# Weight-stationary projections for x, B and C in a hybrid SSD / attention trunk, with edits to the score order and the last product

## The chip, the cores and the metric

One core of one Trainium2 chip runs the whole kernel. The metric is the device time of one execution in microseconds. Three runs of the kernel before gave 2508.55 to 2509.58 us, with a median of 2509.29 us.

## The reference

Two layers over 256 tokens of width 2048, each followed by a SwiGLU feed-forward block; RMSNorm before and after every block, everything in float32.

```python
for i in range(DEPTH):                                   # DEPTH = 2
    h = rmsnorm(x, norm_mix_pre[i])
    if i % 2 == 0:
        m = ssd_mixer(h, ssd_w_in, conv_w, conv_b, dt_bias, a_log, d, norm, w_out)
    else:
        m = diff_attention(h, w_qkv, lq1, lk1, lq2, lk2, subln, w_out, lambda_init)
    x = x + rmsnorm(m, norm_mix_post[i])
    h = rmsnorm(x, norm_ffn_pre[i])
    x = x + rmsnorm((silu(h @ w_gate) * (h @ w_up)) @ w_down, norm_ffn_post[i])
```

`ssd_mixer` multiplies h by `w_in` and cuts the product into a gate z (4096 channels), x (4096), B and C (1024 each) and dt (64). x, B and C go through a causal depthwise convolution of width 4 over the tokens, then SiLU; then a chunked state-space scan, a gated group norm and an output product. `diff_attention` has 16 heads with two score maps each; the second map is subtracted with a weight lambda that comes from four vectors of 64.

## The kernel before, in words

Each matrix product in float32 is made of three float32r products: every operand is split into a high part (`hi`, rounded) and a low part (`lo`, the rest), and hi*hi, hi*lo and lo*hi are added up. Weights stream from memory in blocks of 512 input rows by 512 columns (1 MB); `prep` makes `hi` on ScalarE (a cast, L137) and `lo` on VectorE (a subtraction, L138). In the SSD layer a block is prepared in two halves, with four `hi` and four `lo` buffers in turn; from the attention on, four rows of 512 columns are prepared at once.

Two forms of product matter here.

- `mv` (matmul at L191): the activations are stationary (128 tokens at a time, t = 0 and 1) and the weights stream past, 512 columns at once. A chunk of 512 output columns with 2048 input rows takes 16 x 2 x 3 = 96 matmuls of 512 columns. The result has the tokens on the partitions. The two products of a step run with a lag, so that a chunk's second half of tokens ends inside the next chunk. Two PSUM banks (`acc`, four in all) are used.
- `ws` (matmuls at L239 and L241): the weights are stationary, 128 output channels at a time (`ct` = 0 to 3), and the activations stream: a matmul of 512 columns does hi weights against hi and lo of x for all 256 tokens, a second one of 256 columns does lo weights against hi of x. A chunk takes 16 x 4 = 64 pairs, and the result has the channels on the partitions. All four `acc` banks are used. Evacuation: ScalarE copies one half of the bank out (L1034), VectorE adds the other half (L1035) and, where wanted, multiplies by a row of token scales (L1038). Before the change only q and k of the attention use it.

In the SSD layer (0 to about 616 us) the chunks follow in this order: z0, B0, C0, x0, x1, z1, x2, x3, z2, z3, a first output product, then B1, C1, x4, x5, z4, z5, x6, x7, z6, z7. The twelve chunks of x, B and C go through `conv_chunk`: `mv`, evacuation with the token's scale (`tk`, ScalarE, L515), eight 128x128 transposes on TensorE to bring the channels to the partitions (`pc`, L509), then `conv_silu`, which reads the transposed data from PSUM: ScalarE makes `v` (L492), three scalar_tensor_tensor on VectorE add the shifted taps (L494), ScalarE takes a tanh (L497), VectorE makes the result (L498).

What is not a step of the main product is queued with `later(k, ...)`, which places it k steps further on (a step is half a block, 6 matmuls of each half of the tokens); `tick` runs what is due. The compiler's planner then sets the order on each engine; an engine works in that order. In an attention group, `later` places the scores, the softmax, the turning of the probabilities (transposes, L1091), the weighing of v (L1102) and the turning of the output (`piece`, L326).

At the end, the last product of the second feed-forward block runs as `mv` with the tokens t = 0 four steps ahead of t = 1. `norm_chain` then takes the row sums of squares (L337), a reciprocal root (L94, L97), and adds the scaled result to the residual stream in four pieces of 512 columns (L679, L680, L682), each written out by a DMA of the SP queue (L684).

Of the kernel before, what the change touches and what calls it, by code (L numbers as in the profile page):

```python
# [45 lines left out]
def trunk_kernel(ctx, tc, x_rows, x_cols, vec_cols, vec64, post_rows, lam_rows,  # L46
# [60 lines left out]
    def x_stat(kt, t):  # L107
        sl = slice(t * P, (t + 1) * P)
        return xT_hi[kt // 4][:, kt % 4, sl], xT_lo[kt // 4][:, kt % 4, sl]
# [68 lines left out]
            pending.popleft()()  # L178


    def mv(blocks, stat, evac, lag, scale=None, loaded=()):
        acc = {}
        last = 2 * len(blocks) - 1

        def run(i, t, hi, lo):
# [2 lines left out]
            for j in range(2):
                xh, xl = stat(i, j, t)
                for q, (a, b) in enumerate(((xh, hi), (xh, lo), (xl, hi))):  # L190
                    nc.tensor.matmul(acc[t], a, b[:, j], start=(i == 0 and j == 0 and q == 0),  # L191
                                     stop=(i == last and j == 1 and q == 2))
            if i == last:
# [306 lines left out]
    def conv_chunk(blocks, ch0, dst, then=None):  # L500

        tk = {}

        def conv():
            pcs = [aux("pc").rearrange("p (a s) -> p a s", a=2) for _ in range(2)]
            for t in (1, 0):
                for e, a in ((0, 0), (0, 1), (1, 0), (1, 1)):
# [1 line left out]
                    nc.tensor.transpose(pcs[e][:, a, t * P:(t + 1) * P], tk[t][:, cs], ident)  # L509
            for ct in range(4):  # L510
                conv_silu(pcs[ct // 2][:, ct % 2], ch0 + ct, dst(ct))

        def evac(t, ps):
# [1 line left out]
            nc.scalar.activation(tk[t], ps, AF.Copy, scale=rs0[t])  # L515
# [156 lines left out]
    def norm_chain(t, ss4, last_mw, step, final, t512):  # L672

        rn = rstd_of(ss4[:, 3:4], D, f"post{step}_{t}", ss4[:, 0:1])
        for n in range(4):
# [2 lines left out]
            if final and n == 0:
                nc.scalar.activation(mw, mw, AF.Copy, scale=rn)  # L679
                nc.gpsimd.tensor_tensor(xt, xt, mw, op=ALU.add)  # L680
            else:
                nc.vector.scalar_tensor_tensor(xt, mw, rn, xt, op0=ALU.mult, op1=ALU.add)  # L682
            if final:
                nc.sync.dma_start(out[t * P:(t + 1) * P, n * 512:(n + 1) * 512], xt)  # L684
# [314 lines left out]
    for e in range(2):
        nc.vector.tensor_tensor(lamv[:, 2 * e], lamv[:, 2 * e], lamv[:, 2 * e + 1], op=ALU.mult)  # L1000
        nc.vector.tensor_reduce(lsum[:, e:e + 1], lamv[:, 2 * e], axis=AX.X, op=ALU.add)
    nc.scalar.activation(lsum, lsum, AF.Exp)
# [194 lines left out]
```

## Time and profile before

| | |
|---|---|
| median of 3 runs | 2509.29 us (2508.55 to 2509.58) |
| the profiled execution's own time | 2509.47 us |
| its span | 2507.6 us |
| TensorE busy | 2489.6 us, 11818 matmuls |
| VectorE busy | 1936.8 us |
| ScalarE busy | 1403.2 us |
| GpSimd busy | 263.8 us |
| granted TensorE clock | 0.999 |

The 1.9 us between the span and the execution's own time lie around the program. A matmul's row shows its latency (389 ns for 512 columns), while successive matmuls start about 227 ns apart, so costs on TensorE are read from start to start, or from the chain of waits, which counts each piece once.

### The profile page before, as it was taken

The page shows a single profiled execution, that of the slowest core. Times are in us where ns is not written, and L with a number is a line of the kernel's source. Part 1 is how long each engine was busy: PE and PEld are TensorE (multiplying, and loading weights), DVE is VectorE, ACT ScalarE, POOL GpSimd, SP SyncE. Part 2 cuts the span into 40 slices and gives each one's busy share as a digit, 9 for nine tenths or more (in the row PEclk, how much of TensorE's full clock was granted, in tenths as well). Part 3 has the DMA queues.
Part 4 walks back from the last instruction along what each step waited for, and adds up shares of the span by engine and source line. Part 5 has one row for each costly group of instructions (what it writes and reads, how often), then busy time and mean ns, then how long its engine had stood idle before and what let it go on. Part 6 is the DMA issues. An engine that isn't in the chain of part 4 may idle for free.

```text
span 2507.6 us, 31493 instructions
## 1 busy us (share of the span) xinstructions
PE 2489.6 (99%) x11818; PEld 2062.5 (82%) x11818; DVE 1936.8 (77%) x2394; ACT 1403.2 (56%) x1895; POOL 263.8 (11%) x242
## 2 busy tenths in 40 slices
PE   9999999999999999999999999999999999999998
PEld 8888888888888888888888888888888888888886
DVE  6877547777688899978987766556688899879985
ACT  5767546665565455545554654455655465546553
POOL 0131000121110010001001100001100100020002
PEclk9999999999999999999999999999999999999999
DMA  7555555555786786868676544544776967686774
GB/s 287 195 171 199 185 191 195 175 179 192 255 275 202 253 256 215 256 209 265 217 247 237 185 171 144 199 167 143 255 234 207 289 223 232 217 265 225 224 247 151
DMA packets 143385, 541.43 MB, mean 216 GB/s; under 512 B 14400, under 2 KB 31104, under 8 KB 116224
## 3 DMA queue, kind: packets, MB, share of 16 engines
q1 hardware_dynamic: 125872, 503.96, 57.7%
q0 software_dynamic: 16992, 35.13, 7.1%
q8 instruction: 93, 1.52, 0.2%
q14 instruction: 60, 0.49, 0.1%
q10 hardware_dynamic: 368, 0.32, 0.1%
HBM read 520.41 MB, written 18.94 MB: 215 GB/s over the span
## 4 chain that ended last, share of the span: by engine, by line
PE 93%; DVE 2%; issue 1%; ACT 1%; DMA 1%; POOL 0%; SPq 0%; DVEq 0%; ACTq 0%; POOLq 0%
PE acc L265 38%; PE acc L191 33%; PE cp L265 9%; PE acc L239 5%; PE acc L241 2%; PE acc L216 2%; DVE lo L138 1%; PE pt_f L326 1%; ACT hi L137 1%; DMA raw<-in_w_g_dram 1%; PE py L607 1%; PE ptx L688 0%; PE po L1102 0%; PE pc L509 0%; PE px L594 0%
## 5 line engine op out<-in xcount | busy, mean ns | idle before, releaser
L138 DVE TENSOR_TENSOR lo<-raw,hi 128x2048 fp32r<-128x2048 f32 (+2 forms) x401 | 728.8, 1821 | 307.8 <-ACT hi L137 300.9
L137 ACT CAST hi<-raw 128x2048 fp32r<-128x2048 f32 (+2 forms) x401 | 604.6, 1511 | 432.9 <-PE acc L191 122.7
L191 PE MATMUL acc<-hi,xT 128*128 128x512 f32 x1792 | 570.3, 394 | 0.0
L265 PE MATMUL acc<-hi,xT 128*128 128x512 f32 x1608 | 518.7, 390 | 0.1
L191 PEld LDWEIGHTS acc<-hi,xT 128*128 128x128 f32 x1792 | 336.0, 188 | 71.4 <-issue 2.2
L265 PEld LDWEIGHTS acc<-hi,xT 128*128 128x128 f32 x1608 | 301.8, 188 | 63.0 <-DVE sx L748 0.5
L191 PE MATMUL acc<-lo,xT 128*128 128x512 f32 x896 | 351.9, 393 | 1.4 <-DVE lo L138 1.4
L265 PE MATMUL acc<-lo,xT 128*128 128x512 f32 x804 | 313.0, 389 | 0.0
L138 DVE TENSOR_TENSOR lo<-rawm,hi 128x2048 fp32r<-128x2048 f32 (+1 forms) x87 | 181.8, 2089 | 35.0 <-ACT hi L137 33.7
L137 ACT CAST hi<-rawm 128x2048 fp32r<-128x2048 f32 (+1 forms) x87 | 152.7, 1755 | 95.6 <-PE acc L265 54.6
L191 PEld LDWEIGHTS acc<-lo,xT 128*128 128x128 f32 x896 | 168.4, 188 | 37.3 <-DVE lo L138 4.9
L239 PE MATMUL acc<-xT,hi 128*128 128x512 f32 x512 | 181.2, 399 | 0.0
L265 PEld LDWEIGHTS acc<-lo,xT 128*128 128x128 f32 x804 | 150.9, 188 | 31.2
L265 PE MATMUL acc<-hi,ah_f 128*128 128x512 f32 x450 | 176.1, 391 | 0.0
L265 PE MATMUL acc<-hi,al_f 128*128 128x512 f32 x450 | 175.2, 389 | 0.0
L265 PE MATMUL acc<-lo,ah_f 128*128 128x512 f32 x450 | 175.1, 389 | 0.0
L265 PE MATMUL cp<-sh,ff 128*128 128x512 f32 x516 | 172.8, 389 | 0.0
L241 PE MATMUL acc<-xT,lo 128*128 128x256 f32 x512 | 142.9, 280 | 0.0
L142 DVE SCALAR_TENSOR_TENSOR lo<-raw,cols,hi 128x512 fp32r<-128x512 f32 x128 | 93.5, 774 | 56.9 <-ACT hi L141 56.5
L141 ACT ACTIVATE hi<-raw,cols 128x512 fp32r<-128x512 f32 x128 | 84.7, 716 | 64.1 <-PE acc L191 42.2
L239 PEld LDWEIGHTS acc<-xT,hi 128*128 128x128 f32 x512 | 96.1, 188 | 22.7
L265 PEld LDWEIGHTS cp<-sh,ff 128*128 128x128 f32 x516 | 96.9, 188 | 20.1
(305 smaller groups left out, 4081.5 us busy)
## 6 DMA issues: line engine op xcount, KB each, us to landing
raw<-in_w_zxbc_dram SPq DMA_DIRECT2D x77, 1024.0 KB, 4.8
raw<-in_w_d_dram SPq DMA_DIRECT2D x98, 512.0 KB, 5.8
raw<-in_w_g_dram SPq DMA_DIRECT2D x96, 512.0 KB, 6.5
raw<-in_w_u_dram SPq DMA_DIRECT2D x96, 512.0 KB, 5.9
raw<-in_w_qkv_dram SPq DMA_DIRECT2D x48, 1024.0 KB, 4.8
raw<-in_w_so_dram SPq DMA_DIRECT2D x32, 1024.0 KB, 4.8
rawm<-in_w_g_dram SPq DMA_DIRECT2D x64, 512.0 KB, 5.9
rawm<-in_w_u_dram SPq DMA_DIRECT2D x64, 512.0 KB, 6.1
```

The costliest lines, as they stand in the source:

```text
L137: nc.scalar.copy(hi, raw)
L138: nc.vector.tensor_tensor(lo, raw, hi.bitcast(F32), op=ALU.subtract)
L141: nc.scalar.activation(hi[:, j], raw[:, j], AF.Copy, scale=scale[j])
L142: nc.vector.scalar_tensor_tensor(lo[:, j], raw[:, j], scale[j], hi[:, j].bitcast(F32), op0=ALU.mult, op1=ALU.subtract)
L191: nc.tensor.matmul(acc[t], a, b[:, j], start=(i == 0 and j == 0 and q == 0), stop=(i == last and j == 1 and q == 2))
L216: nc.tensor.matmul(acc[job, t], a, b[:, j], start=(i == 0 and j == 0 and q == 0), stop=(i == last and j == 1 and q == 2))
L239: nc.tensor.matmul(acc[ct], hi[:, j, cs], x.rearrange("p a s -> p (a s)"), start=(i == 0 and j == 0), stop=False)
L241: nc.tensor.matmul(acc[ct][:, :S], lo[:, j, cs], x[:, 0], start=False, stop=(i == last and j == 1))
L265: nc.tensor.matmul(acc[k], a, b, start=first and q == 0, stop=last and q == 2)
L326: nc.tensor.transpose(pt[:, j], src[:, j * P:(j + 1) * P], ident)
L607: nc.tensor.matmul(py[e * 64:(e + 1) * 64, a], xd[c][:, 2 * a + e], mts[c][:, 2 * a + e], start=True, stop=True)
```

## The change

- `conv_chunk` calls `ws` in place of `mv`. Per block of 128 channels, ScalarE copies (`nc.scalar.copy`), VectorE adds and VectorE multiplies by `rstd_bc`, a row of token scales; the eight transposes and the `tk` evacuation go. `conv_silu` reads SBUF, not PSUM, and is queued one step earlier.
- The last product's last pair of K blocks, for t = 1, is split into two halves of 256 columns. What was summed before it is added to `m` first; each half is then evacuated, squared and multiplied on its own.
- At the very end all four pieces of the residual add are made on VectorE (before, the first was made by ScalarE and GpSimd), the last one in two halves, and two of the five DMAs are issued from ScalarE's queue.
- The preparation of lambda is queued 14 steps into the attention.
- In an attention group, the scores are placed one step later in three of the four groups (`k = hg < 3`), the three turnings of the probabilities are placed together, and so are the two weighings.

```diff
+    def mv(blocks, stat, evac, lag, scale=None, loaded=(), cut=False):
...
+            end = cut and i == last and t == 1
+            if end:
+                evac(t, acc[t])
+            for cs in (slice(0, 256), slice(256, 512)) if end else (slice(0, 512),):
+                if end:
+                    acc[t] = accp.tile([P, 512], F32, tag="acc", name="acc")
...
+                if end:
+                    evac(t, acc[t], cs)
...
         def conv():
-            pcs = [aux("pc").rearrange("p (a s) -> p a s", a=2) for _ in range(2)]
-            for t in (1, 0):
-                for e, a in ((0, 0), (0, 1), (1, 0), (1, 1)):
-                    cs = slice((2 * e + a) * P, (2 * e + a + 1) * P)
-                    nc.tensor.transpose(pcs[e][:, a, t * P:(t + 1) * P], tk[t][:, cs], ident)
             for ct in range(4):
-                conv_silu(pcs[ct // 2][:, ct % 2], ch0 + ct, dst(ct))
+                conv_silu(tk[ct], ch0 + ct, dst(ct))
-        def evac(t, ps):
-            tk[t] = s1.tile([P, 512], F32, tag="tk", name="tk")
-            nc.scalar.activation(tk[t], ps, AF.Copy, scale=rs0[t])
-            if t == NT - 1:
+        def evac(ct, ps, pl):
+            if ct % 2 == 0:
+                x = s1.tile([P, 2, S], F32, tag="tk", name="tk")
+                tk.update({ct + e: x[:, e] for e in range(2)})
+            x = tk[ct]
+            nc.scalar.copy(x, pl)
+            nc.vector.tensor_tensor(x, x, ps, op=ALU.add)
+            nc.vector.tensor_tensor(x, x, rstd_bc, op=ALU.mult)
+            if ct == 3:
                 later(1, conv)
...
-        mv(blocks, lambda i, j, t: x_stat(2 * i + j, t), evac, 1)
+        ws(blocks, evac)
...
-            if final and n == 0:
-                nc.scalar.activation(mw, mw, AF.Copy, scale=rn)
-                nc.gpsimd.tensor_tensor(xt, xt, mw, op=ALU.add)
-            else:
-                nc.vector.scalar_tensor_tensor(xt, mw, rn, xt, op0=ALU.mult, op1=ALU.add)
+            for cs in (slice(0, 256), slice(256, 512)) if final and n == 3 else (slice(0, 512),):
+                nc.vector.scalar_tensor_tensor(xt[:, cs], mw[:, cs], rn, xt[:, cs], op0=ALU.mult, op1=ALU.add)
+                if final:
+                    (nc.scalar if n % 2 and not cs.start else nc.sync).dma_start(
...
+            def halfway(t, ps, cs):
+                mt = m[(t, 3)]
+                nc.vector.tensor_tensor(mt[:, cs], mt[:, cs], ps[:, cs], op=ALU.add)
...
+                row_sumsq(sa, mt[:, cs], t512("junk")[:, cs])
...
+                nc.vector.tensor_tensor(last_mw[0][:, cs], mt[:, cs], pw(3)[:, cs], op=ALU.mult)
+                if cs.start:
+                    norm_chain(t, ss4[t], last_mw[0], step, final, t512)
...
+    later(14, lam)
...
-        later(2, all_scores)
-        later(6, lambda: turn(0, (0, 1)))
-        later(8, lambda: (turn(1, (0,)), weigh(0)))
-        later(10, lambda: turn(1, (1,)))
-        later(11, lambda: weigh(1))
-        later(13, lambda: (piece(0), piece(1)))
+        k = hg < 3
+        later(2 + k, all_scores)
+        later(9 + k, lambda: (turn(0, (0, 1)), turn(1, (0,)), turn(1, (1,))))
+        later(10 + k, lambda: (weigh(0), weigh(1)))
+        later(12 + k, lambda: (piece(0), piece(1)))
```

More of the change, by code (lines that the diff above doesn't have):

```diff
@@ L187, in run @@
                 acc[t] = accp.tile([P, 512], F32, tag="acc", name="acc")
[L188 to L193, printed above, removed]
+            end = cut and i == last and t == 1
[4 more added lines that the diff above has]
+                    acc[t] = accp.tile([P, 512], F32, tag="acc", name="acc")
+                for j in range(2):
+                    xh, xl = stat(i, j, t)
+                    for q, (a, b) in enumerate(((xh, hi), (xh, lo), (xl, hi))):
+                        nc.tensor.matmul(acc[t][:, cs], a, b[:, j, cs],
+                                         start=((i == 0 or end) and j == 0 and q == 0),
+                                         stop=(i == last - (cut and t == 1 and not end) and j == 1 and q == 2))
+                if end:
+                    evac(t, acc[t], cs)
+            if i == last and not end:
                 evac(t, acc[t])
@@ L677, in norm_chain @@
             xt = xres[(t, n)]
[L678 to L682 removed]
+            for cs in (slice(0, 256), slice(256, 512)) if final and n == 3 else (slice(0, 512),):
+                nc.vector.scalar_tensor_tensor(xt[:, cs], mw[:, cs], rn, xt[:, cs], op0=ALU.mult, op1=ALU.add)
+                if final:
+                    (nc.scalar if n % 2 and not cs.start else nc.sync).dma_start(
+                        out[t * P:(t + 1) * P, n * 512 + cs.start:n * 512 + cs.stop], xt[:, cs])
             if final:
[L684 removed]
                 continue
@@ L772, in out_proj, with evac @@
                     pw(n)
-            def evac(t, ps, n=n):
+            def halfway(t, ps, cs):
+                mt = m[(t, 3)]
+                nc.vector.tensor_tensor(mt[:, cs], mt[:, cs], ps[:, cs], op=ALU.add)
+                if cs.start == 0:
+                    last_mw.append(t512("mw"))
+                    sa = small.tile([P, 1], F32, tag="ss1", name="ssh", bufs=3)
+                else:
+                    sa = ss4[t][:, 3:4]
+                row_sumsq(sa, mt[:, cs], t512("junk")[:, cs])
+                if cs.start == 0:
+                    nc.vector.scalar_tensor_tensor(ss4[t][:, 0:1], sa, 1.0 / D, ss4[t][:, 0:1], op0=ALU.mult, op1=ALU.add)
+                nc.vector.tensor_tensor(last_mw[0][:, cs], mt[:, cs], pw(3)[:, cs], op=ALU.mult)
+                if cs.start:
+                    norm_chain(t, ss4[t], last_mw[0], step, final, t512)
+            last_mw = []
+            def evac(t, ps, cs=None, n=n):
+                if cs is not None:
+                    return halfway(t, ps, cs)
+                if final and n == 3 and t == 1:
+                    nc.vector.tensor_tensor(m[(t, n)], m[(t, n)], ps, op=ALU.add)
+                    return
                 if first:
@@ L799, in out_proj @@
             mv([w[n, kg // 2] for kg in up[::2]], up_stat, evac, LAG if last and n == 3 else lag,
-               (lambda i: [scale[:, 2 * up[i] + j:2 * up[i] + j + 1] for j in range(2)]) if scale is not None else None)
+               (lambda i: [scale[:, 2 * up[i] + j:2 * up[i] + j + 1] for j in range(2)]) if scale is not None else None,
+               cut=final and n == 3)
     for half in range(2):
@@ L995, in trunk_kernel, with lam @@
     make_causal_mask(nc, causal, NEG)
-    lamv = t512("lamv", (P, 4, 64))
-    nc.scalar.dma_start(lamv, lam_rows.partition_broadcast(P))
     lsum = const.tile([P, 2], F32, name="lsum")
[L999 to L1002, printed above, removed]
     neglam = const.tile([P, 1], F32, name="neglam")
-    nc.vector.tensor_tensor(neglam, lsum[:, 1:2], lsum[:, 0:1], op=ALU.subtract)
-    nc.vector.tensor_scalar(neglam, neglam, -LAMBDA_INIT, None, op0=ALU.add)
+    def lam():
+        lamv = t512("lamv", (P, 4, 64))
+        nc.scalar.dma_start(lamv, lam_rows.partition_broadcast(P))
+        for e in range(2):
+            nc.vector.tensor_tensor(lamv[:, 2 * e], lamv[:, 2 * e], lamv[:, 2 * e + 1], op=ALU.mult)
+            nc.vector.tensor_reduce(lsum[:, e:e + 1], lamv[:, 2 * e], axis=AX.X, op=ALU.add)
+        nc.scalar.activation(lsum, lsum, AF.Exp)
+        nc.vector.tensor_tensor(neglam, lsum[:, 1:2], lsum[:, 0:1], op=ALU.subtract)
+        nc.vector.tensor_scalar(neglam, neglam, -LAMBDA_INIT, None, op0=ALU.add)
+    later(14, lam)
     subc = const.tile([P, 1], F32, name="subc")
```

1 line of the change is left out of this document (removed).

## The prediction

> **What bounds the kernel now.** I read the page first (busy shares, slices, chain), then the chain of waits in one stretch at a time, then the groups by line and shape.
>
> ```profile
> span 2507.6 us, 31493 instructions
> PE 2489.6 (99%) x11818; PEld 2062.5 (82%) x11818; DVE 1936.8 (77%) x2394; ACT 1403.2 (56%) x1895; POOL 263.8 (11%) x242
> ...
> PE 93%; DVE 2%; issue 1%; ACT 1%; DMA 1%; POOL 0%; SPq 0%; DVEq 0%; ACTq 0%; POOLq 0%
> ```
>
> TensorE is the bound from end to end: 93% of the chain, and busy in 2489.6 of 2507.6 us. So a change pays by what it takes off TensorE's own sequence, by a wait on that sequence that it removes, or after the last matmul. All else is hidden as long as VectorE, the next busiest, keeps up. The profiled execution took 2509.47 us (its span and 1.9 us around it), 0.2 above the median of the runs, 2509.29; I make the sum against 2509.47 and take the 0.2 off at the end.
>
> A chunk of the old form and what follows it, in the chain of waits:
>
> ```profile
> 62.06 1.02 PE pc L509 x8
> 63.08 21.82 PE acc L191 x96
> 84.90 0.97 PE pc L509 x8
> ```
>
> The middle row is one whole chunk: 96 matmuls in 21.82 us, 227.3 ns each. The rows beside it are the eight transposes, which cost the path 0.97 to 1.02 us a chunk.
>
> The new form already runs for q and k. The first row below is the chain of a stretch from 1546 to 1630 us, which holds 128 of its pairs; the others are the start and the end of two stretches of pairs, then the group over the run:
>
> ```profile
> by line: PE acc L239 35.7%; PE acc L191 26.6%; PE acc L241 17.8%; DVE lo L138 5.5%; ACT hi L137 4.6%; PE sc L1055 3.2%; PE po L1102 3.2%; PE pp L1091 1.6%; PE pt_o L326 1.0%; DVE sc L1065 0.8%; DVE qk L1038 0.8%; DVE qk L1035 0.8%; issue 0.
> ...
> 1507.38 0.40 PE L239 MATMUL acc<-xT,hi 128*128 128x512 f32 x1
> ...
> 1512.24 0.40 PE L239 MATMUL acc<-xT,hi 128*128 128x512 f32 x1
> ...
> 1514.16 0.40 PE L239 MATMUL acc<-xT,hi 128*128 128x512 f32 x1
> ...
> 1520.17 0.40 PE L239 MATMUL acc<-xT,hi 128*128 128x512 f32 x1
> ...
> L239 PE MATMUL acc<-xT,hi 128*128 128x512 f32 x512 | 181.2, 399 | 0.0
> ```
>
> L239 and L241 hold 53.5% of 84 us, 44.9 us for 128 pairs: 351 ns a pair. The pace has two levels: 14 pairs from 1507.38 to 1512.24 (347 ns) and 17 from 1514.16 to 1520.17 (353.5 ns). TensorE never waited ahead of L239 (idle 0.0), the passage from the q chunk to the k chunk included.
>
> **The change part by part.**
>
> *Transposes out.* Twelve chunks (B and C twice each, x eight times) lose eight transposes each: 12 x 0.97 = -11.7 us, all on the path.
>
> *The new form's pace.* Both forms stream the same columns (96 x 512 = 64 x 768), but a pair takes 351 ns where one and a half old matmuls take 341. A chunk becomes 64 x 0.351 = 22.47 us, 0.65 more: 12 x 0.65 = +7.8 us. By the slower level it is +9.6, by the faster +4.8; I take the mean of the stretch, as the SSD chunks are broken by other work as often as those of q and k.
>
> [...]
>
> *Evacuation.* ScalarE makes four copies (L1034) where it made two scaled ones (L515), 1.49 us for 1.38. VectorE gets four adds and four multiplies more a chunk:
>
> ```profile
> L515 ACT ACTIVATE tk<-acc,rs_in 128x512 f32<-128x512 f32 x24 | 16.5, 690 | 28.8 <-PE acc L191 28.8
> ...
> L1034 ACT COPY qk<-acc 128x256 f32<-128x256 f32 x32 | 11.9, 372 | 19.2 <-PE acc L241 19.2
> ...
> L1035 DVE TENSOR_TENSOR qk<-qk,acc x32: 411/415/422, 1444.7 to 1700.5; 128x256 f32<-128x256 f32 x32
> ...
> L1038 DVE TENSOR_TENSOR qk<-qk,rstd_bc x16: 414/418/427, 1467.7 to 1701.2; 128x256 f32<-128x256 f32 x16
> ...
> 85.00:108.00 23.00, 23.00 (x108) 19.15 (x106) 20.73 (x25) 12.78 (x19) 5.88 (x2) 1.00 0.43 143
> 135.00:161.00 26.00, 26.00 (x152) 21.13 (x152) 22.70 (x42) 21.18 (x42) 7.37 (x5) 1.00 0.65 215
> ...
> PEld acc L191 <- DVE lo L138: 1.1, 5, 0.2
> ...
> 131.29 0.19 PEld L191 LDWEIGHTS acc<-lo,xT 128*128 128x128 f32 x1 [0.23 <-DVE lo L138]
> ```
>
> That is 4 x (0.415 + 0.418) = 3.3 us a chunk, 40 us in all. VectorE (in a window's row after its length, PE and PEld) is busy 20.73 of 23 us in x0's chunk and 22.70 of 26 in z1's, so 3.3 more fills them. What covers it is the four-deep `lo` buffers. That cover is thin where an x chunk meets a z chunk: in the SSD layer TensorE waits for `lo` at five places, four of them at the end of x1, x3, x5 and x7 (the first at 131.29), 0.2 us each. There, work put ahead of `lo` is lost one for one. In favour: in the new form a buffer is held for one step, not one and a half; the scan's work comes a step earlier and meets less of the decay work on ScalarE; and an evacuation may be late without cost, as the idle 0.0 ahead of L239 shows. Bounds: 0, and 4 x 3.3 = +13.3. I take one channel block (0.83) ahead of `lo` at two of the four places, nearer to the waits of 0.2 shown: +1.7 us. The banks (`ws` needs all four, and starts with a flush) I cost at nothing by the same idle 0.0.
>
> *The convolution from SBUF.* A tap on VectorE I leave at its 0.48 us (an all-SBUF one of this size, L1038 above, takes 0.42), but both its tensors are now in SBUF:
>
> ```profile
> 97.03 1.23 DVE L138 TENSOR_TENSOR lo<-raw,hi 128x1024 fp32r<-128x1024 f32 x1 [0.25 <-ACT hi L137]
> ...
> 99.89 5.88 POOL L546 TENSOR_TENSOR mt<-mt,cbm 128x1024 f32<-128x1024 f32 x2 [71.29 <-DVE cbm L554]
> ...
> 103.44 3.42 DVE L138 TENSOR_TENSOR lo<-raw,hi 128x1024 fp32r<-128x1024 f32 x1
> ...
> L494 DVE SCALAR_TENSOR_TENSOR v<-pc,cwh,v x144: 467/476/485, 64.0 to 565.7; 128x253 f32<-128x253 f32 x48, 128x254 f32<-128x254 f32 x48, 128x255 f32<-128x255 f32 x48
> ```
>
> A `lo` of 1.2 us (two SBUF inputs) took 3.42 while GpSimd worked; the 144 taps with one input from PSUM never left 467 to 485 ns. So a tap can now be held up by 2.2 us. GpSimd's long work comes late in the chunks, the taps early, so I cost this at nothing and price it as a rival.
>
> [...]
>
> *Scores one step later, in three groups.*
>
> ```profile
> 1470.67 2.29 DVE L138 TENSOR_TENSOR lo<-raw,hi 128x2048 fp32r<-128x2048 f32 x1 [1.03 <-ACT hi L137]
> ...
> 1473.54 0.41 DVE L1038 TENSOR_TENSOR qk<-qk,rstd_bc 128x256 f32<-128x256 f32 x1
> ...
> 1474.01 1.36 PE L1055 MATMUL sc<-qk 64*128 64x128 f32 x12 [0.70 <-DVE qk L1038]
> ...
> PEld sc L1055 <- DVE qk L1038: 3.5, 4, 0.9
> ```
>
> The scores wait for the last k block, which stood behind a `lo` of 2.29 us: 0.9 us in each of four groups. A step is 12 x 0.227 = 2.7 us, so a step later the block is long done: 3 x 0.9 = -2.7 us; late next is nothing, as the softmax has seven steps. The bound the other way is 0, should the planner move the evacuation back too.
>
> *Turning and weighing together.* The same matmuls; weighing now has one step after three turnings.
>
> ```profile
> 1720.16 1.91 ACT L137 CAST hi<-raw 128x2048 fp32r<-128x2048 f32 x1 [3.14 <-issue]
> 1721.97 0.58 ACT L1093 COPY prT<-pp 128x512 f32<-128x512 f32 x1
> ...
> 1735.37 0.66 PE L326 MATMUL pt_o<-ident,ob 128*128 128x128 f32 x4 [0.31 <-DVE ob L1112]
> ```
>
> Three copies of 0.58 us and one cast of 1.91 make 3.7 us against the step's 2.7 and the turnings' own 1.5 (12 by a pc transpose's 0.12): nothing, at worst +1 a group. In the last group the output is turned two steps after the weighing where one was too short (the third row); that wait goes: -0.4 us with the restart, bounds 0 and -0.5.
>
> *Lambda later.* Its two short products and table load leave the layer's boundary for the q chunk; TensorE waits there for `lo` by 0.27 us:
>
> ```profile
> 1404.45 0.50 PE L191 MATMUL acc<-lo,xT 128*128 128x512 f32 x1 [0.27 <-DVE lo L138]
> ```
>
> In the q chunk TensorE waits for nothing ahead of L239. I cost it at nothing; bounds -0.5 (that wait and its restart) and +0.5 (the same wait in the q chunk).
>
> *The end.*
>
> ```profile
> 2498.09 0.69 DVE L780 TENSOR_TENSOR m<-m,acc 128x512 f32<-128x512 f32 x1 [1.32 <-PE acc L191]
> ...
> 2498.87 0.63 ACT L337 ACTIVATE junk<-m 128x512 f32<-128x512 f32 x1 [4.48 <-DVE m L780]
> ...
> 2500.50 1.42 DVE L682 SCALAR_TENSOR_TENSOR x<-m,rs_post,x 128x512 f32<-128x512 f32 x2 [0.66 <-POOL rs_post L97]
> 2501.30 1.74 POOL L680 TENSOR_TENSOR x<-x,m 128x512 f32<-128x512 f32 x1 [0.83 <-ACT m L679]
> 2501.83 1.75 DVE L682 SCALAR_TENSOR_TENSOR x<-mw,rs_post,x 128x512 f32<-128x512 f32 x1
> ...
> 2496.24 8.12 SPq L684 DMA_DIRECT2D out_dram<-x  x7
> ...
> DMA to landing us min/median/max: 2.0/2.1/2.4
> ```
>
> With half the columns left after the last matmul, the add takes 0.42 for 0.69 (L1035's shape) and the square about 0.4 for 0.63: 0.5 us sooner. The five adds on VectorE, with GpSimd quiet, take 3 x 0.7 + 2 x 0.4 from 2500.0 and end at 2502.8; now the last ends at 2503.58, stretched to 1.75 beside GpSimd, and the SP queue waits for GpSimd's piece until 2503.04 and then issues three DMAs in a row. The last DMA goes out some 1.1 us sooner and lands in the 2.0 of the row, not 2.4: -1.4 us; bounds -0.5 (the halves alone) and -1.6. The 12 short matmuls for 6 long ones cost under 0.1.
>
> Sum: -11.7 + 7.8 + 1.7 - 2.7 - 0.4 - 1.4 = -6.7 us, so 2502.8 for this execution and 2502.6 beside the median.
>
> **The rivals.**
>
> 1. *VectorE eats the gain* (the same within 0.2%). At each of the four places half of the chunk's new work, 1.65 us, lies ahead of `lo`: +6.6 for +1.7, 2507.5. For it: the five waits and the windows near 90%. Against: the taps start a step earlier and the buffers are held shorter.
> 2. *VectorE becomes the bound of the SSD layer* (slower). All 3.3 us and one hold-up of 2.2 by GpSimd fall ahead of `lo` at the four places: 4 x 5.5 = +22 for +1.7, 2522.9. It decides from 3.4 us a place, where the loss of 13.4 outweighs the other terms (-8.4) by 5. For it: the `lo` of 3.42. Against: GpSimd is busy 5.88 of 23 us there, and hardly while the taps run.
> 3. *The pace costs nothing*: in the SSD chunks the weight loads hide wholly, a pair takes 1.5 x 227 = 341 ns, and the +7.8 goes: 2494.8. [...] Against: not one of the two levels, 347 and 353.5.
> 4. *The change doesn't do what it says*: the pace is at the slow level (+9.6) and the scores' wait moves with them (0), leaving -11.7 + 9.6 + 1.7 - 0.4 - 1.4 = -2.2: 2507.1. For it: most of the q and k pairs run at 353.5.
>
> **How the numbers follow.** The forecast has 0.55, with its own range 2498 to 2504 (the pace's bounds, and 0 to 3 us for VectorE). Rival 1 has 0.25, rival 2 0.09, rival 3 0.03, rival 4 0.08. A difference of under 0.2%, 5 us, is about what a measurement of this kernel can't tell from none: faster (under 2504.3) is the forecast and rival 3, 0.58; the same is rivals 1 and 4, 0.33; slower 0.09. The range 2496 to 2510 leaves out rivals 2 and 3 and the far side of rival 1.
>
> **What would show it.** No pc transposes; L239 and L241 with 1280 pairs at 347 to 354 ns; waits of TensorE for `lo` in the SSD layer of 1 to 4 us in total (over 10 is rival 2); L494 near 480 ns, with a few over 2 us if GpSimd holds it; the wait of the scores for qk once, not four times; last matmul to span's end 8.1 us, not 9.5. The prediction is wrong if TensorE's gaps in the SSD layer grow by more than 4 us, or if a pair runs outside 345 to 356 ns.

## The result and the profile after

The change makes the kernel slower: 2528.59 us median (2528.21 to 2533.32) beside 2509.31 for the kernel before on the same chip, ratio 1.0081, 95% interval 1.0070 to 1.0091. The prediction said 2502.6. The profiled execution after took 2529.99 us, its span 2528.2, 20.6 more than before.

Where the 20.6 us lie is read from the first transposes (`ptx`) behind the first mixer, the first feed-forward block and the second mixer, which part the run into four stretches: the SSD layer, the first feed-forward block, the attention and the rest. Three rows of before, then the same three of after, from the timelines of TensorE:

```profile
687.16 0.63 PE L688 MATMUL ptx<-ident,x 128*128 128x128 f32 x4 [0.66 <-issue]
...
1392.21 0.66 PE L688 MATMUL ptx<-ident,x 128*128 128x128 f32 x4 [0.60 <-DVE x L682]
...
1789.56 0.63 PE L688 MATMUL ptx<-ident,x 128*128 128x128 f32 x4 [0.70 <-DVE x L682]
```

```profile
712.92 0.63 PE L696 MATMUL ptx<-ident,x 128*128 128x128 f32 x4 [0.66 <-issue]
...
1418.15 0.66 PE L696 MATMUL ptx<-ident,x 128*128 128x128 f32 x4 [0.61 <-DVE x L688]
...
1811.52 0.63 PE L696 MATMUL ptx<-ident,x 128*128 128x128 f32 x4 [0.70 <-DVE x L688]
```

The SSD layer lost 25.8 us (prediction: -2.2 = -11.7 + 7.8 + 1.7). The first feed-forward block lost 0.2. The attention took 393.4 us for 397.4, -4.0 (prediction: -3.1), and the last stretch, from 1811.52 to the span's end, 716.7 for 718.0, -1.4 (prediction: -1.4). So all that is wrong lies in the SSD layer. The page first:

```profile
span 2528.2 us, 32250 instructions
...
PE 2493.3 (99%) x12112; PEld 2079.2 (82%) x12112; DVE 1974.2 (78%) x2498; ACT 1405.6 (56%) x1919; POOL 262.1 (10%) x240
```

TensorE is still the bound, with 294 matmuls more and 3.7 us more of busy time: 17 of the 20.6 us are time in which it stood still. The waits of TensorE for VectorE from 0 to 711 us (total, times, longest), the only row over 0.3 us before and then the rows after:

```profile
PE acc L191 <- DVE lo L138: 0.8, 2, 0.5
```

```profile
PE acc L197 <- DVE tk L523: 13.9, 4, 3.5
PE acc L248 <- DVE tk L523: 6.4, 4, 2.0
...
PE acc L197 <- DVE lo L138: 0.7, 2, 0.5
```

TensorE now waits 20.3 us for the add of the evacuation (L523; from `mv` on, the lines of the changed kernel are 6 to 35 higher): four times 3.5 us where x1, x3, x5 and x7 meet `mv`, and four times up to 2.0 where x0, x2, x4 and x6 meet the next `ws`. It does not wait for `lo`, as the prediction's rivals had it, but for the bank that the add empties; the prediction had called itself wrong if these gaps grew by more than 4 us. The timeline at the end of x1 shows why the add is late:

```profile
127.23 0.43 DVE L563 TENSOR_TENSOR cbm<-pcb,tri 128x256 f32<-128x256 f32 x1
...
127.80 5.74 POOL L555 TENSOR_TENSOR mt<-mt,cbm 128x1024 f32<-128x1024 f32 x2 [1.26 <-DVE cbm L563]
128.09 7.67 DVE L138 TENSOR_TENSOR lo<-raw,hi 128x1024 fp32r<-128x1024 f32 x3
130.77 0.37 ACT L522 COPY tk<-acc 128x256 f32<-128x256 f32 x1
...
132.40 0.28 PE L250 MATMUL acc<-xT,lo 128*128 128x256 f32 x1
...
135.68 0.74 DVE L523 TENSOR_TENSOR tk<-tk,acc 128x256 f32<-128x256 f32 x2
136.14 0.79 PE L197 MATMUL acc<-hi,xT 128*128 128x512 f32 x1 [3.47 <-DVE tk L523]
```

ScalarE begins to copy the first bank's other half at 130.77, so the bank is ready to be emptied. The add stands behind three `lo` in VectorE's order. They take 7.67 us, not three times 1.22 = 3.7. GpSimd's two decay multiplies (L555) run from 127.80 to 133.54, and one by one the rows are:

```profile
127.80 2.41 POOL L555 TENSOR_TENSOR mt<-mt,cbm 128x1024 f32<-128x1024 f32 x1 [1.26 <-DVE cbm L563]
...
128.09 3.21 DVE L138 TENSOR_TENSOR lo<-raw,hi 128x1024 fp32r<-128x1024 f32 x1
...
130.16 3.38 POOL L555 TENSOR_TENSOR mt<-mt,cbm 128x1024 f32<-128x1024 f32 x1
131.22 3.40 DVE L138 TENSOR_TENSOR lo<-raw,hi 128x1024 fp32r<-128x1024 f32 x1
...
134.54 1.21 DVE L138 TENSOR_TENSOR lo<-raw,hi 128x1024 fp32r<-128x1024 f32 x1
```

The two `lo` that begin beside a multiply take 3.21 and 3.40 us, the one that begins after them 1.21; in e14, which leaves the multiplies out, the same three take 2.36 (two) and 1.23 us. "Lock-out" stands below for this longer time of `lo` beside GpSimd's multiply; what makes it so inside the chip no run shows. The add starts at 135.68; `mv`, which needs the same bank, has waited since 132.68.

A second loss stands behind five of the eight waits. Windows of after (length, PE, PEld, DVE, ACT, POOL, then the granted clock): the wait at x1, what follows it at x1, x3, x5 and x7, and what follows x6:

```profile
132.60:136.10 3.50, 0.08 (x1) 0.00 (x0) 3.50 (x4) 1.32 (x2) 0.94 (x1) 0.93 0.11 28
136.10:141.00 4.90, 4.86 (x18) 3.71 (x19) 4.90 (x12) 1.09 (x2) 0.00 (x0) 0.70 0.72 254
222.90:229.00 6.10, 6.06 (x21) 4.39 (x22) 6.10 (x15) 1.99 (x4) 0.00 (x0) 0.72 0.77 290
463.90:471.00 7.10, 7.00 (x20) 5.16 (x21) 7.10 (x18) 2.10 (x4) 0.00 (x0) 0.56 0.80 299
575.40:582.00 6.60, 6.46 (x24) 4.68 (x25) 6.60 (x17) 1.99 (x4) 0.00 (x0) 0.74 0.81 313
...
545.20:548.61 3.41, 3.41 (x12) 2.94 (x12) 3.41 (x9) 0.88 (x2) 0.00 (x0) 0.50 0.32 38
```

Before, the clock was 1.00 at x1's end (its row for 129 to 145 us is below). After, it is 0.56 to 0.74 for 5 to 7 us behind each of the four long waits, and 0.50 for 3.4 us behind one of the four shorter ones, x6's. At full clock the work of these windows would have taken up to 4.9 x 0.30 + 6.1 x 0.28 + 7.1 x 0.44 + 6.6 x 0.26 + 3.4 x 0.50 = 9.7 us less, an estimate. Waits of 20.3 and up to 9.7 of slow clock make 30.0. The layer lost 25.8 where the transposes and the pace alone (-11.7 + 7.8) would have given -3.9, which is 29.7 more.

```profile
129.00:145.00 16.00, 16.00 (x77) 12.50 (x77) 13.44 (x23) 9.77 (x17) 3.42 (x4) 1.00 0.73 249
```

### The profile page after: what moved, and what is told of

Read it like the earlier page. It is cut to its first block, busy times and chain, and to the rows that moved or that the text cites. A ratio compares the mean times of both kernels' runs of the same rounds, so it can differ in the third digit from the quotient of the medians.

```text
span 2528.2 us, 32250 instructions
## 1 busy us (share of the span) xinstructions
PE 2493.3 (99%) x12112; PEld 2079.2 (82%) x12112; DVE 1974.2 (78%) x2498; ACT 1405.6 (56%) x1919; POOL 262.1 (10%) x240
## 4 chain that ended last, share of the span: by engine, by line
PE 94%; DVE 3%; issue 1%; DMA 1%; ACT 1%; POOL 0%; DVEq 0%; POOLq 0%; SPq 0%; ACTq 0%
PE acc L274 38%; PE acc L197 25%; PE acc L248 11%; PE cp L274 9%; PE acc L250 6%; DVE lo L138 2%; PE acc L225 2%; PE pt_f L335 1%; PE py L616 1%; PE ptx L696 0%; DMA raw<-in_w_g_dram 0%; ACT hi L137 0%; PE po L1137 0%; PE sc L1090 0%; PE pyo L644 0%
## 5 line engine op out<-in xcount | busy, mean ns | idle before, releaser
L138 DVE TENSOR_TENSOR lo<-raw,hi 128x2048 fp32r<-128x2048 f32 (+2 forms) x401 | 740.3, 1851 | 291.2 <-ACT hi L137 286.9
L274 PE MATMUL acc<-hi,xT 128*128 128x512 f32 x1608 | 518.9, 390 | 0.3 <-DVE sx L756 0.3
L248 PE MATMUL acc<-xT,hi 128*128 128x512 f32 x1280 | 454.1, 399 | 6.4 <-DVE tk L523 6.4
L250 PE MATMUL acc<-xT,lo 128*128 128x256 f32 x1280 | 356.9, 280 | 0.0
L274 PEld LDWEIGHTS acc<-hi,xT 128*128 128x128 f32 x1608 | 301.8, 188 | 63.3 <-DVE sx L756 0.7
L197 PE MATMUL acc<-hi,xT 128*128 128x512 f32 x1024 | 330.5, 397 | 14.0 <-DVE tk L523 13.9
L274 PE MATMUL acc<-lo,xT 128*128 128x512 f32 x804 | 313.0, 389 | 0.0
L248 PEld LDWEIGHTS acc<-xT,hi 128*128 128x128 f32 x1280 | 240.5, 188 | 63.9 <-DVE tk L523 8.0
L250 PEld LDWEIGHTS acc<-xT,lo 128*128 128x128 f32 x1280 | 242.2, 189 | 1.3
L197 PEld LDWEIGHTS acc<-hi,xT 128*128 128x128 f32 x1024 | 193.6, 189 | 57.2 <-DVE tk L523 15.2
L197 PE MATMUL acc<-lo,xT 128*128 128x512 f32 x512 | 202.3, 396 | 1.2 <-DVE lo L138 1.2
L274 PEld LDWEIGHTS acc<-lo,xT 128*128 128x128 f32 x804 | 151.0, 188 | 31.3
L197 PEld LDWEIGHTS acc<-lo,xT 128*128 128x128 f32 x512 | 97.0, 189 | 22.4 <-DVE lo L138 4.0
```

Of the source, the lines that this page charges most:

```text
L138: nc.vector.tensor_tensor(lo, raw, hi.bitcast(F32), op=ALU.subtract)
L197: nc.tensor.matmul(acc[t][:, cs], a, b[:, j, cs], start=((i == 0 or end) and j == 0 and q == 0), stop=(i == last - (cut and t == 1 and not ...
L248: nc.tensor.matmul(acc[ct], hi[:, j, cs], x.rearrange("p a s -> p (a s)"), start=(i == 0 and j == 0), stop=False)
L250: nc.tensor.matmul(acc[ct][:, :S], lo[:, j, cs], x[:, 0], start=False, stop=(i == last and j == 1))
L274: nc.tensor.matmul(acc[k], a, b, start=first and q == 0, stop=last and q == 2)
```

## The experiments

The theory: the loss needs both the new chunk (an add on VectorE that releases a PSUM bank) and GpSimd's multiply across the chunk's end. Rivals: VectorE simply has too much work; the reordering elsewhere; the planner's new order on VectorE; the hand-over of four banks as such. Each ratio is to the kernel before on the same chip. The kernel before took 2509.3 to 2509.8 us (medians) beside each set of runs, so the text compares times across the sets.

| label | kernel | us | ratio, 95% interval |
|---|---|---|---|
| e1_conv_only | before + new chunk | 2533.44 | 1.0081 to 1.0111 |
| e2_rest_only | after, old chunk | 2504.37 | 0.9969 to 0.9989 |
| e4_decay_dve | after, multiply on VectorE | 2506.18 | 0.9977 to 0.9996 |
| e5_before_decay_dve | before, multiply on VectorE | 2509.20 | 0.9988 to 1.0007 |
| e6_copy_both | after, ScalarE empties the banks | 2521.85 | 1.0034 to 1.0064 |
| e7_cb_earlier | after, product C B a step earlier | 2511.23 | 0.9995 to 1.0014 |
| e8_fill | after, idle products in the waits | 2526.83 | 1.0053 to 1.0083 |
| e9_cb_earlier_dve | e4 and e7 together | 2502.54 | 0.9958 to 0.9982 |
| e10_all_earlier | e7, whole decay a step earlier | 2512.41 | 1.0001 to 1.0019 |
| e11_before_later | before, decay a step later | 2510.30 | 0.9994 to 1.0012 |
| e12_bc_only | e2, new chunk for B and C only | 2502.79 | 0.9962 to 0.9983 |
| e13_split | after, multiply split over both engines | 2510.78 | 0.9993 to 1.0013 |
| e14_no_multiply | after, multiply left out | 2499.46 | 0.9944 to 0.9974 |
| e15_rest_cb_dve | e2 with e9's edits | 2504.89 | 0.9972 to 0.9990 |

**Which part costs: e1 and e2.** One has the new `conv_chunk` alone, the other all but it.

```diff
 # e1, on the kernel before
...
-        mv(blocks, lambda i, j, t: x_stat(2 * i + j, t), evac, 1)
+        ws(blocks, evac)
...
 # e2, on the kernel after: the same two lines the other way, with the old evac and transposes
```

> The kernel before with the new conv_chunk alone (weights stationary, no transposes); scores, turning and end as before. Theory (a PSUM bank of ws is held because the evacuation's add L523 stands on VectorE behind locked `lo` and decay work; the stall of 3.6 us then drops the granted clock): here the scan's order is also unchanged, so the loss of +25.8 us measured in the SSD layer stays and the attention's and the end's gains (-4.0 and -1.0) are missing: 2509.3 + 26 = 2535, or less if the later turn/scan step kept the decay away from the x chunk's end. Rival (the reordering of the SSD tail or of the scores costs the time): 2503 to 2510.

> The changed kernel with the old conv_chunk (tokens stationary, transposes, conv from PSUM); scores, turning and the end stay changed. Theory: only the gains of attention (-4.0) and end (-1.0) are left: 2504, ratio 0.998. Rival (the loss comes from work that moved in the rest): 2525 and more.

Measured 2533.44 and 2504.37: +24.1 and -5.0, together +19.1 for the whole change's +19.3. The reordering rival is out. The parts outside the SSD layer gain 5.0 us; the prediction had 4.5 (2.7 + 0.4 + 1.4).

**The multiply's engine: e4, and its control e5.**

```diff
-        nc.gpsimd.tensor_tensor(mt, mt, cbm[:, c]..., op=ALU.mult)
+        nc.vector.tensor_tensor(mt, mt, cbm[:, c]..., op=ALU.mult)
```

> The changed kernel with the decay multiply (L555, 128 x 1024, twice per x chunk) on VectorE instead of GpSimd. Theory: the lock-out is what makes `lo` late (3 in 7.67 us instead of 3.7), so `lo` takes 3.7 us again, but VectorE has two more products of some 1.2 us per x chunk to do; the waits at the add shrink from 3.6 us to 1 or 2 and the clock stays up: 2506 to 2516. Rival (VectorE is simply over-full, the lock-out is beside the point): two more products per x chunk make it slower, 2530 to 2548.

> The kernel before with the decay multiply (L546) on VectorE instead of GpSimd: the control to the same edit on the changed kernel, which took that from 2528.6 to 2506.2. Theory (GpSimd's lock-out costs only where a PSUM bank waits in VectorE's queue): the banks of before are not held in that queue (ScalarE empties them), so the edit gives within 4 us of 2509.3. Rival (the edit saves some 20 us in any kernel, and the gain says nothing of the bank): 2490 or so.

Measured 2506.18 and 2509.20. VectorE has more to do in e4 than in the kernel after (16 multiplies of 1.22 us), and the kernel is 22.4 us faster; in the kernel before the same edit gives nothing. So it is not VectorE's sum of work alone, and not GpSimd's multiply alone: it is the multiply on GpSimd together with the new chunk.

**Is it the bank alone: e6.** ScalarE copies both halves, and VectorE's add reads SBUF (a small tile of the set-up gives up its room for the third buffer). With two buffers of its own for `xs` (e3) the pool needs 27.5 KB a partition where 26.5 are left.

```diff
...
-            nc.vector.tensor_tensor(x, x, ps, op=ALU.add)
+            xs = s1.tile([P, S], F32, tag="v", name="xs", bufs=3)
+            nc.scalar.copy(xs, ps)
+            nc.vector.tensor_tensor(x, x, xs, op=ALU.add)
```

> The changed kernel with ScalarE copying both halves of an accumulator out of PSUM and VectorE adding from SBUF; the decay multiply stays on GpSimd. Three of four banks then come free whatever stands in VectorE's queue. Theory (the bank is the wait): the 20.3 us of idle TensorE behind the add goes, and with it some 5.8 us of cold clock; what can be late next is `lo` itself behind the same lock-out, by 0 to 1.5 us at four places: 2502 to 2510. Rival (VectorE's queue is late by 3.6 us in all, so `lo` takes the place of the add): 2522 to 2530.

Measured 2521.85: only 6.7 us came back of the 19 to 27 expected, and here the theory fell short. The wait at the add is gone, but another takes its place twelve microseconds after the hand-over, inside the z chunk (and TensorE waits 4.2 us in all at `px`, for the convolution's result, where it was 0.3 after). The waits of TensorE for `lo`, the late matmul in the timeline, and the window around it:

```profile
PE acc L197 <- DVE lo L138: 11.9, 7, 2.7
```

```profile
150.28 0.50 PE L197 MATMUL acc<-lo,xT 128*128 128x512 f32 x1 [2.72 <-DVE lo L138]
```

```profile
130.00:150.00 20.00, 17.57 (x87) 14.21 (x85) 20.00 (x37) 13.07 (x28) 6.59 (x3) 1.00 0.55 184
```

VectorE is busy 20.00 of 20 us there: it has no slack in that stretch, so the 4 us that the lock-out takes (7.67 - 3.7) are paid, at the bank or at a later `lo`.

**Where the lock-out falls: e7, e10, e11.**

```diff
 # e7, on the kernel after
-        later(6, lambda: products_cb(g, st))
+        later(5, lambda: products_cb(g, st))
 # e10: e7, and decay_load at later(3), decay at later(5 + c)
 # e11, on the kernel before: products_cb at later(7), decay at later(7 + c)
```

> The changed kernel with the product C B (which the decay multiply waits for, through cbm) one step earlier, later(5) for later(6), nothing else: GpSimd's multiplies can begin at some 121 and 125 us of the span instead of 127.8 and 130.6, ahead of the last `lo` of the x chunk. Theory (it is where the lock-out falls, not how long it is): most of the wait behind the add goes: 2505 to 2515. Rival (VectorE's sum of work decides): 2526 to 2530.

> The changed kernel with the whole decay work one step (2.8 us) earlier: its loads later(3), the product C B later(5), the decay later(5) and later(6); the multiply stays on GpSimd, as long as ever. Theory (what counts is whether the lock-out lies across the `lo` and adds at the x chunk's end): the multiplies end some 2 us before they did with the product alone moved (2511.2, waits of 9.1 us left), so another 3 to 6 us go: 2505 to 2508. Rival (the lock-out costs VectorE's queue the same wherever it lies): 2511 or more.

> The kernel before with the product C B and the decay one step later (later(7), later(7) and later(8) for 6, 6 and 7), so that the lock-out lies across the end of the x chunk as it does in the changed kernel; ScalarE still empties the banks. Theory (the lock-out at the chunk's end makes `lo` late whoever empties the bank, as the 2.7 us at `lo` showed where ScalarE copied both halves): waits at `lo` at four to eight places, 2512 to 2522. Rival (tokens-stationary with its evacuation on ScalarE is proof against it): 2507 to 2511.

e7 measured 2511.23: 17.4 us back with the same instructions on the same engines. Its waits at the add:

```profile
PE acc L197 <- DVE tk L523: 7.5, 4, 2.0
PE acc L248 <- DVE tk L523: 1.6, 3, 0.7
```

e10 measured 2512.41, no better than e7, but it did not do what its text assumed. Its timeline:

```profile
123.41 5.74 POOL L555 TENSOR_TENSOR mt<-mt,cbm 128x1024 f32<-128x1024 f32 x2 [19.00 <-DVE cbm L563]
```

The multiplies wait for `cbm`, which hangs on the product C B that e7 had moved already; only the loads and ScalarE's part moved. It tells nothing of a still earlier lock-out.

e11 measured 2510.30, and there my theory lost: the kernel before is proof against it. In its timeline GpSimd's multiplies and the longer `lo` stand at the end of x1 as they do after:

```profile
128.90 5.76 POOL L546 TENSOR_TENSOR mt<-mt,cbm 128x1024 f32<-128x1024 f32 x2
130.07 2.32 DVE L138 TENSOR_TENSOR lo<-raw,hi 128x1024 fp32r<-128x1024 f32 x1
...
132.77 2.96 DVE L138 TENSOR_TENSOR lo<-raw,hi 128x1024 fp32r<-128x1024 f32 x1 [0.38 <-ACT hi L137]
```

Two `lo` take 1.1 and 1.7 us over their 1.22, and yet this is all that TensorE waits for `lo` from 0 to 735 us:

```profile
PE acc L191 <- DVE lo L138: 0.8, 2, 0.5
```

Without the new evacuation (3.3 us a chunk) VectorE has slack to take the delay: it is busy 18.72 of the 20 us from 130 to 150 here, where it was 20.00 in e6. That this slack is the reason is argued, not tested.

**The clock: e8.**

```diff
         ws(blocks, evac)
+        if then and ch0 // 4 % 2:
+            pf = aux("pfill")
+            x = xT[0][:, 0]
+            for _ in range(14):
+                nc.tensor.matmul(pf, x[:, 0, :P], x.rearrange("p a s -> p (a s)"), start=True, stop=True)
```

> The changed kernel with 14 idle products of 128x512 (3.2 us, into a spare bank, read by nobody) issued by TensorE behind the last pair of x1, x3, x5 and x7, where it otherwise stands still for 3.5 us. They take the place of idle time alone. Theory: the granted clock stays at 1.00 behind the four places, so the 5.8 us that the matmuls there lose now is saved and the wait stays: 2528.6 - 5.8 = 2523, range 2520 to 2526. Rival (the products behind the wait are slow for want of operands or for the burst of DMA, not of the clock): 2528 to 2530.

Measured 2526.83, 1.8 us under the kernel after, and the two intervals overlap: inconclusive as a time. The windows say more, behind x1 and then behind x0, where nothing was filled in:

```profile
139.10:144.00 4.90, 4.62 (x22) 3.57 (x23) 4.90 (x13) 1.10 (x2) 0.00 (x0) 1.00 0.72 237
...
109.50:113.50 4.00, 4.00 (x16) 3.38 (x16) 4.00 (x9) 0.46 (x1) 0.00 (x0) 0.62 0.53 147
```

With TensorE kept busy the clock behind the wait is 1.00 (0.70 after), with the same burst of transfers (0.72): the slowness is the clock, not the transfers. The clock is 1.00 behind x3, x5 and x7 too. But in this execution the wait of 2.0 us at x0 was followed by 0.62, where the clock was 1.00 after, and a `lo` came late by 2.1 us. What the clock costs in all stays open, between the 1.8 us that came back here, not clear of the noise, and the 9.7 above.

**Order or lock-out: e14 and e13.** In e4, e6, e7 and e9 the planner also set `lo` and add in another order. e14 leaves the multiply out, and VectorE's instructions stand in exactly the order of the kernel after; e13 gives four heads to each engine.

```diff
 # e14
-        nc.gpsimd.tensor_tensor(mt, mt, cbm[:, c]..., op=ALU.mult)
 # e13
-        nc.gpsimd.tensor_tensor(mt, mt, cbm[:, c]..., op=ALU.mult)
+        for eng, hs in ((nc.gpsimd, slice(0, 4)), (nc.vector, slice(4, 8))):
+            eng.tensor_tensor(mt[:, hs], mt[:, hs], cbm[:, c]..., op=ALU.mult)
```

> The changed kernel without the decay multiply, so the scores' mask and C B factor are left out of the scan's weights. VectorE's instructions stand in the very order of the changed kernel, three `lo` ahead of the add included; only the lock-out is gone. Theory: the three `lo` take 3.7 us and the add is in time: no wait at the add, 2501 to 2505. Rival (the planner's order by itself keeps the banks, and the kernels with the multiply on VectorE gained by their other order): 2515 to 2528.

> The changed kernel with each decay multiply parted: GpSimd takes four of the eight heads, VectorE the other four. Half the lock-out. Theory (the loss is the time that VectorE is locked out while it has no slack, less what its slack takes): the delay at the add was 3.5 us of some 4.2 us of lock-out at four places, 1.6 us at the other four; half the lock-out leaves 0 to 1.4 us at each place and half a product more on VectorE: 2505 to 2513. Rival (the planner's order, with three `lo` ahead of the add, costs the time by itself): 2525 or more.

e14 measured 2499.46, 29.1 us under the kernel after. The same place in its timeline, then its only row of waits for VectorE over 0.5 us:

```profile
127.42 2.36 DVE L138 TENSOR_TENSOR lo<-raw,hi 128x1024 fp32r<-128x1024 f32 x2
130.18 0.37 ACT L522 COPY tk<-acc 128x256 f32<-128x256 f32 x1
130.32 1.23 DVE L138 TENSOR_TENSOR lo<-raw,hi 128x1024 fp32r<-128x1024 f32 x1 [0.54 <-ACT hi L137]
...
131.46 0.75 DVE L523 TENSOR_TENSOR tk<-tk,acc 128x256 f32<-128x256 f32 x2
131.93 0.50 PE L197 MATMUL acc<-hi,xT 128*128 128x512 f32 x1
```

```profile
PE acc L197 <- DVE lo L138: 1.3, 4, 0.5
```

Three `lo` still stand ahead of the add, and cost nothing: TensorE passes to `mv` with no wait. The planner's order is out as a cause by itself. e13 measured 2510.78, with half the waits:

```profile
PE acc L197 <- DVE tk L523: 5.6, 4, 1.7
PE acc L248 <- DVE tk L523: 2.6, 3, 0.9
PE acc L197 <- DVE lo L138: 2.5, 4, 1.6
```

Whole, half and no multiply on GpSimd: 21.0, 10.7 and 1.3 us of waits for VectorE, 2528.6, 2510.8 and 2499.5 us. (In e13 VectorE's halves ran beside GpSimd's and its order had two `lo` ahead of the add, so it is no pure half.)

**The hand-over, and what the new chunk is worth: e12, e9, e15.** e12 calls `ws` in `bc_chunk` alone; e9 has the edits of e4 and e7; e15 has them with the old chunk.

```diff
 # e12, on e2 (conv_chunk_ws is the conv_chunk of the kernel after)
-        conv_chunk([w_zxbc[16 + 2 * which + half, k] for k in range(4)], ...)
+        conv_chunk_ws([w_zxbc[16 + 2 * which + half, k] for k in range(4)], ...)
 # e9, on after, and e15, on e2
-        later(6, lambda: products_cb(g, st))
+        later(5, lambda: products_cb(g, st))
-        nc.gpsimd.tensor_tensor(mt, mt, cbm[:, c]..., op=ALU.mult)
+        nc.vector.tensor_tensor(mt, mt, cbm[:, c]..., op=ALU.mult)
```

> Weights stationary for the four chunks of B and C alone, where no decay multiply runs on GpSimd; the eight x chunks as before; scores, turning and the end as changed (2504.4 without any weights-stationary chunk). Theory: a third of the transposes' 11.7 less a third of the pace's 7.8 is gained and nothing waits: 2504.4 - 1.3 = 2503. Rival (each weights-stationary chunk costs 2 us by the handing over of four banks, lock-out or not): 2511.

> The changed kernel with both edits: the product C B one step earlier, and the decay multiply on VectorE. Theory: with the lock-out gone and VectorE's two products (2 x 1.22 us) ahead of the last `lo` of the x chunk, the waits behind the add and the 5.6 us at `lo` that were left with the multiply on VectorE alone go too: 2506.2 - 4 = 2502, what the prediction's sum had. Rival (the 5.6 us at `lo` are one late transfer of weights and have nothing to do with it): 2506.

> The control to the fastest so far (2502.5: the changed kernel with the product C B a step earlier and the multiply on VectorE): both edits with the old conv_chunk, scores, turning and end as changed. Theory: the two edits give nothing where the evacuation is on ScalarE, so 2504.4 as without them, and the weights-stationary chunks are worth 2 us by themselves. Rival (the two edits make any version faster): 2502 or less, and the weights-stationary chunks are worth nothing.

e12 measured 2502.79, 1.6 under e2 (expected 1.3; the intervals overlap) and far from the rival's 2511: four chunks hand over their banks for nothing where GpSimd has no multiply. e9 measured 2502.54, the lowest median but for e14 (not clear of e12's), 7.2 under the kernel before beside it and 26 under the kernel after. What is left of its waits for VectorE:

```profile
PE acc L197 <- DVE lo L138: 2.9, 4, 1.9
```

e15 measured 2504.89, no gain from the two edits on the old chunk. So with the lock-out out of the way the medians put the twelve new chunks at -2.35 us (e15 to e9; these intervals overlap as well, by 0.001); the prediction's three terms had -2.2.

## Why the prediction was wrong

**The step that failed** is in the evacuation: "The banks (`ws` needs all four, and starts with a flush) I cost at nothing by the same idle 0.0", and "an evacuation may be late without cost, as the idle 0.0 ahead of L239 shows". The banks cost 20.3 us of waits, and up to 9.7 of slow clock behind them. The row of L239 was right, but it came from the attention, where the condition that makes the add late hardly exists. Windows of the kernel before, in the q and k chunks and in the SSD layer (GpSimd's is the fifth of the busy times):

```profile
1440.00:1560.00 120.00, 118.61 (x675) 101.02 (x675) 74.82 (x115) 59.67 (x104) 2.06 (x2) 1.00 0.48 167
100.00:220.00 120.00, 120.00 (x639) 97.53 (x638) 93.38 (x141) 80.70 (x147) 36.76 (x19) 1.00 0.56 187
```

GpSimd is busy 2.06 of 120 us where the row was taken, and 36.76 where it was applied; VectorE 74.82 and 93.38.

**The lock-out was seen and given to the wrong instruction.** The prediction quoted a `lo` of 3.42 us, and asked only whether a tap would be held up. The taps were as it said, with one hold-up of 0.35 us at most:

```profile
L503 DVE SCALAR_TENSOR_TENSOR v<-tk,cwh,v x144: 469/476/825, 62.3 to 588.2; 128x253 f32<-128x253 f32 x48, 128x254 f32<-128x254 f32 x48, 128x255 f32<-128x255 f32 x48
```

But `lo` was locked out before already (3.42 us at 103.44 in the kernel before), and what was new is what stands behind it: the add, with a bank that TensorE waits for.

**Rival 2 came nearest, but by another path.** It had the place (the four ends of odd x chunks), GpSimd's hold-up and roughly the price: 22 us at 5.5 a place, where 13.9 at 3.5 was measured. But it had TensorE wait for `lo`, by over 10 us; the wait for `lo` was 0.7 and the one for the bank 20.3. It had nothing at the even ends (6.4) and nothing of the clock, and its reason, VectorE's sum of work, does not do it by itself (e4). That its 2522.9 lies so near the measured time is in part chance. It was weighed against by "GpSimd is busy 5.88 of 23 us there, and hardly while the taps run": a share, where the place in the queue decides.

**What held.** Transposes and pace: e14, without the lock-out, ends its SSD layer at 683.01 (the same `ptx` row as in the result) for 687.16, -4.15; the two terms were -11.7 + 7.8 = -3.9 (12 x 0.97 is 11.6, which changes nothing). As e14 lacks the multiply's work too, this is no pure measure of them: e9, which has that work on VectorE, ends the layer at 685.98, -1.2. The pace itself is 0.353 us a pair over six pairs of x1's chunk, the rows below, and 0.346 over fourteen later ones (127.31 to 132.16):

```profile
121.74 0.40 PE L248 MATMUL acc<-xT,hi 128*128 128x512 f32 x1
...
123.86 0.40 PE L248 MATMUL acc<-xT,hi 128*128 128x512 f32 x1
```

The scores wait once, not four times. The attention gained 0.9 us more than forecast; one wait of 0.3 for `lo` fewer is part of that, and the rest stays open. The end is 2528.2 - 2519.92 = 8.3 us behind the last matmul, where it was 2507.6 - 2498.05 = 9.55 (predicted 8.1 for 9.5). The rows are the waits of TensorE's weight loads for the scores in the attention, then the last matmul of after and of before:

```profile
PEld sc L1090 <- DVE qk L1073: 0.9, 1, 0.9
```

```profile
2519.64 0.28 PE L197 MATMUL acc<-hi,al_f 128*128 128x256 f32 x1
```

```profile
2497.66 0.39 PE L191 MATMUL acc<-hi,al_f 128*128 128x512 f32 x1
```

So apart from the one step the sum stands within about 1 us a term, and e9, in which that step's cost is gone, takes 2502.54 where 2502.6 was predicted; since the multiply then stands on VectorE, that they agree to 0.1 us is partly chance.

## What to carry to other kernels

An idle time of 0.0 read in one stage is evidence for that stage only: before it prices an edit elsewhere, compare what the other engines do there. Moving the release of a PSUM bank from ScalarE's queue (busy 80.70 of 120 us in the SSD layer before) into VectorE's (93.38) made everything ahead of it in that queue, and everything that slowed these instructions, part of TensorE's path: 20.3 us of waits here. And where an edit adds work to an engine with no slack, look in the timeline for instructions that take longer beside a second engine's (here `lo`, 3.40 us for 1.21): moving 16 multiplies to the engine that was already the busier one gained 22 us.

## What the runs showed of the hardware

In the trace of after, up to its last matmul at 2519.64 us, the granted clock was 0.50 in five stretches, four of 3.41 us and one of 6.83, and 1.00 elsewhere. They begin at 135.60, 224.34, 463.28, 545.20 and 575.92 us, and these starts lie 26, 70, 24 and 9 times 3.413 us apart. The rows are the five stretches, then the 3.41 us ahead of each:

```profile
135.60:139.01 3.41, 2.87 (x7) 2.29 (x8) 3.41 (x9) 1.09 (x2) 0.00 (x0) 0.50 0.80 307
224.34:227.76 3.41, 3.41 (x12) 2.17 (x11) 3.41 (x8) 0.34 (x1) 0.00 (x0) 0.50 0.67 226
463.28:470.11 6.83, 6.10 (x17) 4.38 (x17) 6.83 (x17) 2.09 (x4) 0.00 (x0) 0.50 0.78 277
545.20:548.61 3.41, 3.41 (x12) 2.94 (x12) 3.41 (x9) 0.88 (x2) 0.00 (x0) 0.50 0.32 38
575.92:579.33 3.41, 3.41 (x8) 2.13 (x7) 3.41 (x9) 1.09 (x2) 0.00 (x0) 0.50 0.78 293
...
132.19:135.60 3.41, 0.49 (x4) 0.17 (x2) 3.41 (x2) 1.52 (x3) 1.36 (x1) 1.00 0.00 0
220.93:224.34 3.41, 1.40 (x6) 1.19 (x7) 3.41 (x8) 0.75 (x2) 0.00 (x0) 1.00 0.60 178
459.87:463.28 3.41, 0.67 (x4) 0.30 (x3) 3.41 (x2) 1.69 (x3) 1.53 (x1) 1.00 0.00 0
541.78:545.20 3.41, 1.40 (x9) 0.98 (x8) 3.41 (x5) 1.77 (x4) 1.08 (x1) 1.00 0.16 65
572.50:575.92 3.41, 0.38 (x2) 0.34 (x3) 3.41 (x5) 0.86 (x2) 0.43 (x1) 1.00 0.14 36
```

In the 3.41 us ahead of them TensorE stood still (the length less PE's busy time) for 2.92, 2.01, 2.74, 2.01 and 3.03 us. With the whole trace up to the last matmul parted in the same way, the most among the parts at 1.00 that no 0.50 follows is 1.82 us, from 432.56:

```profile
432.56:435.97 3.41, 1.59 (x9) 1.42 (x10) 3.41 (x7) 1.98 (x4) 0.36 (x1) 1.00 0.02 10
435.97:439.38 3.41, 3.41 (x22) 2.99 (x21) 3.41 (x9) 0.93 (x2) 0.00 (x0) 1.00 0.40 115
```

Two other runs, parted so, stand beside it. In e7 TensorE stood still for 1.82 us behind x3 within one such part, and the next had 0.50. In e1 a wait of 3.47 us at the same place fell into two parts, 1.75 and 1.72 us; both had 1.00, and so had 190 to 235 us as a whole. The rows are e7's part and the one behind it, then e1's two:

```profile
214.09:217.50 3.41, 1.59 (x9) 1.15 (x8) 3.41 (x7) 2.05 (x4) 0.00 (x0) 1.00 0.23 46
217.50:220.92 3.42, 3.42 (x8) 2.29 (x8) 3.42 (x9) 1.09 (x2) 0.00 (x0) 0.50 0.78 285
...
221.81:225.22 3.41, 1.66 (x10) 1.21 (x8) 3.41 (x2) 2.19 (x5) 2.52 (x1) 1.00 0.00 0
225.22:228.63 3.41, 1.69 (x7) 1.42 (x8) 3.41 (x8) 1.04 (x2) 0.00 (x0) 1.00 0.57 192
```

So in these rows the length of the single wait does not tell whether a 0.50 follows. Within one part, 2.01 to 3.03 us in after and 1.82 us in e7 had one behind them, and 1.82 us in after had none; the 3.47 us over two parts in e1 had none. No run was made to show what sets the clock.
